# The attention projection as a third Strassen turn, and raw weight loads issued from GpSimd

## Chip, cores and metric

One core of a Trainium2 chip. The metric is the device time of one execution in microseconds (us). Engines: TensorE (PE), VectorE (DVE), ScalarE (ACT), GpSimd (POOL), and SyncE (SP), which issues DMAs.

## The reference

A decoder layer on 512 tokens of width 2048, in float32. Two branches read the normalised and modulated input: an attention over a sliding window (32 heads of 64), and a gated delta rule (32 value heads of 128). Cut to what matters here:

```python
    y_a = a_out @ w_o_swa                               # [512, 2048] @ [2048, 2048]
    ...
    y_b = o.reshape(B, T, DN_VAL).astype(x.dtype) @ w_o_dn   # [512, 4096] @ [4096, 2048]
    y = jax.nn.sigmoid(mg_a) * y_a + jax.nn.sigmoid(mg_b) * y_b
    return x + gate * (y @ w_out)                       # [512, 2048] @ [2048, 2048]
```

## The kernel before

**Precision.** Each float32 operand is split into a high part (a ScalarE cast, L61) and the rest (a VectorE subtraction, L62), and each product is three matmuls (`mm3`, L273 to L275). So a 128x128 by 128x512 step costs three matmuls.

**Weights.** All weights pass PE once, as a list of jobs of 1 MB (`plan`). A job is loaded into a raw buffer (`load_job`, L215), split in two halves of 128x1024 (`split_half`, tiles whi and wlo, three buffers of each), and used. A half that is done frees its buffer; at the next step (`pump`) the split of a further half and the load of a further job are put into the program.

**Order.** The program is written out in the order of PE's work. Beside it run generators: `go` steps one after so many pumps, `paced` steps one by a budget: each pump adds the budget, each step costs what it yields. The compiler then orders the instructions of each engine by this order and by when it expects them to be ready. `behind` keeps an instruction from being ordered ahead of the last matmul put in before it.

**Stages.** Start and norm; delta keys; attention; delta heads (16 of them, 40 pumps each, then three tiles of the merge gate); four more tiles of the merge gate; then the closing stages, which the change touches:

- *Delta projection* (`branch_b`). [512, 4096] times [4096, 2048] is taken as two turns (h = 0, 1) over halves of the inner width, each a [512, 2048] x [2048, 2048] product by one level of Strassen (Winograd's form): for each of two column halves n, seven products m1, m7, m5, m2, m6, m4, m3 (`PRODUCTS`). Each is four weight halves by two token blocks by two by three matmuls, 48 in all. It needs sums of quarters of the activations (the forms a11, s3, s1, a12, s2, a22, s4, each a pair of tiles of 8 KB per partition, in slots f0 to f4 and x0 to x3) and sums of quarters of the weights. `delta_forms` makes forms from `o_d`, direct into slots or by way of `b_d` and `form_load`. `delta_evict` combines the products on VectorE; the first turn stores to `yo_d`, the second adds `prev` from there, transposes each [128 tokens, 512] block by four PE transposes into `pty` (L320), multiplies with the gate (`th`, from `mb_d`) and stores to `yb_d`.
- *Weight sums* (`weight_sums`): the sums of quarters of w_o_dn (two sets, to `g_d`) and of w_out (one set, to `f_d`), paced beside the delta heads from head 3 on, with budget 2.0. Of each set, every half quarter takes four loads of 512 KB, four adds of 128x1024 on VectorE (L1328) and four stores.
- *Attention projection* (first part of `finish`): `attention_input` loads `ao_d` and splits it into hh and hl during the second turn; then 16 tiles of 128 channels by 512 tokens (`channel_tile`, 16 x 3 matmuls each, jobs os0 to os15). Each is gated with `ma_d`, `yb_d` is added, and the forms of the output projection are made from it in the same layout.
- *Output projection* (`output`): again seven products for each column half, then gate, residual and store. In PSUM the products rotate over six banks, and m7 has two.

All DMAs go out from SP, in the order of its instructions; a raw load waits on SP until its buffer is free. Raw buffers: two (`wraw`) and one more in the od jobs (`braw`), three more in the output projection (`oraw`). A raw load is L215; loads of prev and th are L1290 and L1293, of o L1204 and L1205.

Of the kernel before, what the change touches and what calls it, by code (L numbers as in the profile page):

```python
# [45 lines left out]
class Layer:  # L46
# [104 lines left out]
    def plan(self):  # L151
# [42 lines left out]
    def prime(self):  # L194
        self.job_load = self.half_split = self.half_used = 0
        self.raws, self.halves, self.due = {}, {}, []
        self.paused = False
# [4 lines left out]
    def load_job(self):  # L202
        j = self.job_load
        if j < len(self.jobs):
            src = self.jobs[j][1]
            if j == self.od1 and not self.paused:
                self.paused = True
                return
            if self.od0 <= j < self.od1:
                own = (j - self.od0) % 3 < 2  # L210
            else:
                own = j < self.out0 or (j - self.out0) % 5 < 2
            pool, tag = (self.wraw, "raw") if own else (self.oraw, "rawo")
            raw = pool.tile([P, 2048], F32, tag=tag, name="raw")
            self.nc.sync.dma_start(out=raw[:, : src.shape[-1]], in_=src)  # L215
# [107 lines left out]
    def build(self):  # L323
        tc, nc, a = self.tc, self.nc, self.a
        with ExitStack() as es:
# [6 lines left out]
            self.g_d = self.dram.tile([2, 2, 4, 2, P, 2048], F32, name="g_d")  # L332
# [22 lines left out]
            self.yb_d = self.dram.tile([KT, P, T], F32, name="yb_d")  # L355
# [6 lines left out]
            self.y_d = self.dram.tile([KT, P, T], F32, name="y_d")  # L362
# [3 lines left out]
            self.branch_b(work)  # L366
            self.finish(es, work, pm_es)
# [332 lines left out]
    def delta_heads(self):  # L700
        tc, nc = self.tc, self.nc
        with ExitStack() as sb:
# [423 lines left out]
    def branch_b(self, wk):  # L1126
        tc, nc, a = self.tc, self.nc, self.a
        forms = [p[1] for p in PRODUCTS]
        self.b_d = self.dram.tile([2, 2, P, 8, T], F32, name="b_d")
        self.yo_d = self.dram.tile([4, 4, P, T], F32, name="yo_d")  # L1130
        with ExitStack() as es:
            pf = self.pmb
            w = lambda name: wk.tile([P, T], F32, tag="w", name=name, bufs=9)
            self.gwk, self.gtag = wk, "w"
            fm = es.enter_context(tc.tile_pool(name="bf", bufs=1, side="right", reuse_waits="tile"))
            slots = [tuple(fm.tile([P, 8, 256], F32, name=f"f{i}{x}").bitcast(F32R) for x in "hl") for i in range(5)]
            fm.tile([P, 8], F32, name="alignb")
            self.oraw = es.enter_context(tc.tile_pool(name="braw", bufs=1, side="right", reuse_waits="tile"))
            A = [dict(zip(forms, slots)), {}]
# [5 lines left out]
            hx = ExitStack()  # L1145
            fx = hx.enter_context(tc.tile_pool(name="bx", bufs=1, reuse_waits="tile"))
            more = [tuple(fx.tile([P, 8, 256], F32, name=f"x{i}{x}").bitcast(F32R) for x in "hl") for i in range(4)]
            A[0].update(zip(forms[5:], more))
            for i, f in enumerate(forms[5:]):
                self.go(self.form_load(0, f, A[0][f]), 2 + 12 * i)  # L1150
            A[1].update(zip(forms, more[2:]))
            build = self.paced(self.delta_forms(wk, w, 1, A[1], 1), 1.0)
            ps, keep = {}, {}
            items = [(h, n, m) for h in range(2) for n in range(2) for m in range(7)]
            for h, n, m in items:
                name, form = PRODUCTS[m][:2]
                if (h, n, m) == (0, 1, 3):
                    self.drain_slow(build)
                k = [(0, 1, 3), (0, 1, 4), (0, 1, 5), (0, 1, 6), (1, 0, 0)]
                if (h, n, m) in k:  # L1160
                    k = k.index((h, n, m))
                    A[1][forms[k + 2]] = slots[k]
                    self.go(self.form_load(1, forms[k + 2], slots[k]), 2)
                if (h, n, m) == (1, 1, 2):
                    hx.close()
                    self.h_es = ExitStack()
                    self.hpool = self.h_es.enter_context(tc.tile_pool(name="h2", bufs=1))
                    self.hh = self.hpool.tile([P, KT, T], F32R, name="hh")
                    self.hl = self.hpool.tile([P, KT, T], F32R, name="hl")
                    ao = self.paced(self.attention_input(w), 1.0)  # L1170
                for t in range(2):
                    m7 = name == "m7"
                    ps[name, t] = pf.tile([P, T], F32, tag=f"y{t}", name=name, bufs=1) if m7 else self.product_bank(name)
                ah, al = A[h][form]
                for p in range(4):
                    hi, lo = self.half(f"od{h}{n}_{m}_{p // 2}")
                    for t in range(2):
                        for k in range(2):
                            kt, cols, tsl = 2 * p + k, slice(k * T, k * T + T), slice(t * P, (t + 1) * P)
                            self.mm3(ps[name, t], (ah[:, kt, tsl], al[:, kt, tsl]), (hi[:, cols], lo[:, cols]), kt == 0, kt == 7)  # L1180
                        if t:
                            self.half_done()
                        self.pump()
# [706 lines left out]
```

## Time and profile before

| | |
|---|---|
| time, median of 3 runs | 2791.58 us (2791.4 to 2793.72) |
| the profiled execution | 2789.26 us, of which the span 2787.2 us |
| granted TensorE clock | 0.999 |
| moved by DMA | 603.4 MB, mean 216 GB/s |
| second turn ends, attention projection starts | 2452.3 us |
| attention projection ends, output projection starts | 2630.3 us |

How to read the profile. In a list of stretches a row gives the stretch, its length, then for PE, PEld (weight load of PE), DVE, ACT and POOL the busy time and instructions, then the granted clock, the busy share of the DMA engines, and GB/s. In a list by tile or line a row gives line, engine, operation, output<-inputs and count; then either the least, median and longest duration in ns and the first and last start, or the busy time, the mean ns of one, and the idle time before with what ended it. Buffer numbers are left out of the names of rotating tiles (m is m1 to m7). A row of waits gives who waited for whom: us in all, times, and the longest. A timeline row gives start, duration, engine, line and operation, and in brackets the idle time before.

### The profile page before, as it was taken

To read this page: it belongs to the slowest core of one execution; us is meant where nothing else is said; L and a number is where in the kernel's file an instruction comes from. 1 tells how busy PE (TensorE), PEld (TensorE's weight loads), DVE (VectorE), ACT (ScalarE), POOL (GpSimd) and SP (SyncE) were. 2 spreads that over 40 slices of the span, in tenths; PEclk is the share of its full clock that TensorE was granted. 3 is DMA by queue.
4 is the path that set the end of the run, shared out by engine and by line. 5 is a ranking of instruction groups with operands and counts; after the bars stand their busy time and mean duration, and the time that the engine had idled before them with its cause. 6 is when DMAs were issued, how large, how long until landed. Compare 5 with 4: busy or idle time off the path is not lost.

```text
span 2787.2 us, 38923 instructions
## 1 busy us (share of the span) xinstructions
PE 2759.0 (99%) x14410; PEld 2256.5 (81%) x14410; DVE 1957.9 (70%) x3285; ACT 1207.4 (43%) x2508; POOL 137.9 (5%) x124
## 2 busy tenths in 40 slices
PE   8999999999999999999999999999999999999999
PEld 5788888877777788888888888888888888878887
DVE  7866986877758667788766666666657776764676
ACT  5555443244544433444534444444435454423443
POOL 0011110100100010000000000000000000000000
PEclk9999999999999999999999999999999999999999
DMA  9878764322253253367787776767647887885784
GB/s 403 353 235 243 269 229 131 112 93 93 87 144 112 101 166 116 116 214 243 258 268 242 241 243 242 239 235 248 227 162 266 310 298 245 284 272 189 245 315 168
DMA packets 228993, 603.40 MB, mean 216 GB/s; under 512 B 76706, under 2 KB 103074, under 8 KB 188482
## 3 DMA queue, kind: packets, MB, share of 16 engines
q1 hardware_dynamic: 228804, 600.93, 63.4%
q8 instruction: 113, 1.85, 0.3%
q14 instruction: 76, 0.62, 0.1%
HBM read 480.38 MB, written 118.24 MB: 215 GB/s over the span
## 4 chain that ended last, share of the span: by engine, by line
PE 90%; DMA 3%; DVE 3%; ACT 1%; issue 1%; SPq 0%; POOL 0%; DVEq 0%; POOLq 0%; ACTq 0%
PE mm L273 22%; PE mm L275 22%; PE mm L274 21%; PE m L274 5%; PE m L275 5%; PE m L273 5%; PE pod L1082 1%; PE pv L1063 1%; PE O L1597 1%; PE pp L1053 1%; PE pod L1078 1%; PE pod L1081 1%; DVE wlo L62 1%; DMA gw<-in_w_ada_gate 1%; DMA prev<-yo_d 1%
## 5 line engine op out<-in xcount | busy, mean ns | idle before, releaser
L273 PE MATMUL mm<-hh,whi 128*128 128x512 f32 x2784 | 1118.2, 402 | 0.0
L275 PE MATMUL mm<-hh,wlo 128*128 128x512 f32 x2784 | 1087.2, 391 | 1.9 <-DVE wlo L62 1.9
L274 PE MATMUL mm<-hl,whi 128*128 128x512 f32 x2784 | 1086.4, 390 | 0.0
L62 DVE TENSOR_TENSOR wlo<-raw,whi 128x1024 fp32r<-128x1024 f32 x516 | 636.1, 1233 | 463.8 <-ACT whi L61 450.7
L61 ACT CAST whi<-raw 128x1024 fp32r<-128x1024 f32 x516 | 541.1, 1050 | 884.2 <-PE mm L274 638.2
L273 PEld LDWEIGHTS mm<-hh,whi 128*128 128x128 f32 x2784 | 523.4, 188 | 115.4 <-issue 11.8
L275 PEld LDWEIGHTS mm<-hh,wlo 128*128 128x128 f32 x2784 | 522.5, 188 | 113.4 <-DVE wlo L62 2.5
L274 PEld LDWEIGHTS mm<-hl,whi 128*128 128x128 f32 x2784 | 523.5, 188 | 103.0 <-issue 1.4
L809 ACT ACTIVATE E<-E,neg_g 128x128 f32<-128x128 f32 x256 | 81.5, 391 | 99.3 <-POOL E L803 97.4
L1328 DVE TENSOR_TENSOR q<-q,q 128x1024 f32<-128x1024 f32 x96 | 120.1, 1251 | 1.4 <-DMA q<-in_w_od 1.4
L847 DVE TENSOR_TENSOR A<-A,atmp 128x62 f32<-128x62 f32 (+30 forms) x124 | 109.2, 881 | 0.4
L839 DVE TENSOR_TENSOR atmp<-A 128x62 f32<-128x62 f32 (+30 forms) x124 | 106.6, 860 | 0.4
L992 POOL TENSOR_TENSOR qe<-qe,yq 128x512 f32<-128x512 f32 x32 | 51.8, 1632 | 893.2 <-DMA qe<-eg_rows 553.2
L652 DVE SCALAR_TENSOR_TENSOR yv<-mm,convh,yv 128x511 f32<-128x511 f32 (+2 forms) x96 | 71.4, 744 | 10.2 <-ACT yv L649 9.5
L803 POOL TENSOR_SCALAR_AFFINE_SELECT E<-E 128x512 f32<-128x512 f32 x64 | 54.7, 863 | 436.5 <-DMA E<-g_rows 359.5
L1083 ACT COPY osb<-pod 128x256 f32<-128x256 f32 x64 | 23.7, 370 | 96.9 <-PE pod L1082 96.9
L1565 ACT ACTIVATE sm<-sm,mx,rs 128x128 f32<-128x128 f32 x128 | 61.5, 482 | 4.8 <-DVE mx L1560 4.4
L1065 ACT COPY vn<-pv 128x256 f32<-128x256 f32 x64 | 23.6, 369 | 73.0 <-PE pv L1063 73.0
L1056 DVE SCALAR_TENSOR_TENSOR r<-pp,neg_eg,vt 128x128 f32<-128x128 f32 x96 | 29.2, 345 | 34.3 <-PE pp L1053 34.1
L472 DVE SCALAR_TENSOR_TENSOR wa<-wa,silu_cb 128x2048 f32<-128x2048 f32 x22 | 50.1, 2285 | 2.6 <-DMA wa<-in_w_ada_ss 2.6
L657 ACT ACTIVATE th<-yv 128x512 f32<-128x512 f32 x32 | 20.2, 632 | 70.6 <-DVE yv L652 70.5
L1082 PE MATMUL pod<-vn,E 128*128 128x128 f32 x256 | 46.8, 275 | 0.0
(449 smaller groups left out, 3610.7 us busy)
## 6 DMA issues: line engine op xcount, KB each, us to landing
raw<-in_w_ch SPq DMA_DIRECT2D x158, 1024.0 KB
wa<-in_w_ada_ss SPq DMA_DIRECT2D x32, 1024.0 KB
q<-in_w_od SPq DMA_DIRECT2D x64, 512.0 KB
g_d<-q SPq DMA_DIRECT2D x64, 512.0 KB
raw<-g_d SPq DMA_DIRECT2D x32, 1024.0 KB
raw<-in_w_od SPq DMA_DIRECT2D x24, 1024.0 KB
gw<-in_w_ada_gate SPq DMA_DIRECT2D x16, 1024.0 KB
E<-g_rows SPq DMA_DIRECT2D x64, 256.0 KB
```

Of the source, the lines that this page charges most:

```text
L61: h = self.nc.scalar.copy(out=hi, in_=src)
L62: l = self.nc.vector.tensor_tensor(out=lo, in0=src, in1=hi.bitcast(F32), op=ALU.subtract)
L273: nc.tensor.matmul(ps, lhsT=wh, rhs=xh, start=first, stop=False)
L274: nc.tensor.matmul(ps, lhsT=wh, rhs=xl, start=False, stop=False)
L275: self.last_mm = nc.tensor.matmul(ps, lhsT=wl, rhs=xh, start=False, stop=last)
L652: nc.vector.scalar_tensor_tensor(out=y[:, s:], in0=ps[:, : T - s], scalar=w[:, j : j + 1], in1=y[:, s:], op0=ALU.mult, op1=ALU.add)
L809: self.nc.scalar.activation(E[:, c, :], E[:, c, :], AF.Exp, bias=self.neg_g[:, c, h : h + 1])
L839: eng.tensor_tensor(out=t, in0=A[:, m : m + 1, m + 1 :].to_broadcast([P, m, n]), in1=A[:, :m, m : m + 1].to_broadcast([P, m, n]), op=ALU.mult,
L847: self.behind(eng.tensor_tensor(out=A[:, :m, m + 1 :], in0=A[:, :m, m + 1 :], in1=t, op=ALU.add))
L1082: nc.tensor.matmul(po[:, e, :], lhsT=M[e][:, c, :], rhs=vn[:, e, :], start=c == 0, stop=True)
L1328: self.behind(nc.vector.tensor_tensor(out=q[f], in0=q[x], in1=q[y], op=ALU.add))
L1565: nc.scalar.activation(t, t, AF.Exp, scale=r[:, h : h + 1], bias=mx[:, h : h + 1], accum_out=den[:, h : h + 1])
```

## The change

The attention projection becomes a third turn (h = 2) of the delta projection: the same product loops, with weights w_o_swa and the forms made by `delta_forms` from `ao_d`. `branch_b` is now `projections`, and calls `output` at its end; `finish` and `attention_input` are gone. The third turn's blocks come out as [tokens, 512] and go through a new generator, `y_blocks`, which transposes, gates and adds as above and makes the forms of the output projection: written straight into slots where those are free, else stored to `c_d` and fetched with `y_half`. `weight_sums` has a fourth set (w_o_swa to `g_d[2]`), starts at head 1 with budget 1.0 and goes on with 2.4 from head 3. From the third od job on, raw loads are issued from GpSimd. In the second turn the loads of prev and th go out for both blocks at once, and four pumps pass before their use. The output projection takes its PSUM banks from the four that the turns use, and has two raw buffers of its own in place of three.

```diff
@@ plan
-        for half in range(2):
+        for half in range(3):
...
-        self.od1 = len(jobs)
-        jobs += [(f"os{j}", a["w_os"][j]) for j in range(KT)]
@@ load_job
-            if j == self.od1 and not self.paused:
-                self.paused = True
-                return
-            if self.od0 <= j < self.od1:
+            if j < self.od0:
+                own = True
+            elif j < self.out0:
                 own = (j - self.od0) % 3 < 2
             else:
-                own = j < self.out0 or (j - self.out0) % 5 < 2
-            pool, tag = (self.wraw, "raw") if own else (self.oraw, "rawo")
+                own = (j - self.out0) % 5 < 2
+            third = j < self.out0 or (j - self.out0) % 5 == 2
+            pool, tag = (self.wraw, "raw") if own else (self.braw if third else self.oraw, "rawo")
             raw = pool.tile([P, 2048], F32, tag=tag, name="raw")
-            self.nc.sync.dma_start(out=raw[:, : src.shape[-1]], in_=src)
+            (self.nc.sync if j < self.od0 + 3 else self.nc.gpsimd).dma_start(out=raw[:, : src.shape[-1]], in_=src)
...
-            if j == self.od0 + 1:
+            if j in (self.od0 + 1, self.out0 + 2, self.out0 + 3):
                 self.load_job()
@@ delta_heads
+                if g == 1:
+                    sums = self.paced(self.weight_sums(ws), 1.0)
                 if g == 3:
-                    sums = self.paced(self.weight_sums(ws), 2.0)
+                    sums[1] = 2.4
@@ branch_b -> projections
+            A[2].update(zip(forms, more[:2]))
+            A[3].update(zip(forms, slots[3:]))
+            places = {1: slots, 2: more[2:] + slots[:3]}
+            taken = {(2, 1, 1): ("s1", more[0]), (2, 1, 2): ("a12", more[1])}
+            taken.update({(2, 1, 5): ("s2", slots[0]), (2, 1, 6): ("a22", slots[1])})
...
+                        if h < 2 and (n, m) == (0, 0):
+                            build = self.paced(self.delta_forms(wk, w, h + 1, A[h + 1], 1), 1.0)
...
+                        if (h, n, m) in taken:
+                            self.y_half(*taken[h, n, m])
...
+            self.output(w, fx, A[3], slots[2])
+    def y_half(self, f, slot):
+        self.ydst[f] = slot
+        self.go(self.form_load(self.c_d[self.cforms.index(f)], slot, 4), 2)
@@ delta_evict
+        if h == 2:
+            yield from self.y_blocks(wk, w, pf, n, name, out)
+            return
+        loads = []
+        for c, t, src in out if h else ():
...
+        if loads:
+            yield 4
...
-            yield 3
             TT(out=src, in0=src, in1=prev, op=ALU.add)
...
-            nc.sync.dma_start(out=self.yb_d[4 * cc : 4 * cc + 4, :, tsl].rearrange("j p t -> p j t"), in_=th)
+            nc.sync.dma_start(out=self.yb_d[cc, t], in_=th.rearrange("p j t -> p (j t)"))
@@ y_blocks
+        for c, t, src in out:
...
+        yield 4
+        for t, src, y, b in blocks:
+            pt = pf.tile([P, 4, P], F32, tag="tp", name="pty", bufs=2)
+            self.transpose4(pt.rearrange("p j t -> p (j t)"), lambda j: src[:, j * P : (j + 1) * P])
+            yield 1
+            STT(out=y, in0=y, scalar=1.0, in1=pt.rearrange("p j t -> p (j t)"), op0=ALU.add, op1=ALU.mult)
+            TT(out=y, in0=y, in1=b, op=ALU.add)
+        yield 1
+        def put(f, t, src):
+            tsl = slice(t * P, (t + 1) * P)
+            if f in self.ydst:
+                ks = slice(4 * n, 4 * n + 4)
+                self.split(self.ydst[f][0][:, ks, tsl], self.ydst[f][1][:, ks, tsl], four(src))
+            else:
+                nc.sync.dma_start(out=self.c_d[self.cforms.index(f)][:, :, tsl], in_=four(src))
...
@@ weight_sums
-        sets = [(a["w_od"][0], self.g_d[0]), (a["w_od"][1], self.g_d[1]), (a["w_out"], self.f_d)]
+        sets = [(a["w_od"][h], self.g_d[h]) for h in range(3)] + [(a["w_out"], self.f_d)]
@@ output
-                    ps[name, t] = pf.tile([P, T], F32, tag=f"y{t}" if m7 else "r", name=name, bufs=1 if m7 else 6)
+                    ps[name, t] = pf.tile([P, T], F32, tag=f"y{t}", name=name, bufs=1) if m7 else self.product_bank(name)
...
-            if n == 0 and m in (2, 3):
-                kt = 4 * (m - 2) + p
-                nc.sync.dma_start(out=late[:, kt], in_=self.c_d[kt])
+            if (n, m, p) == (0, 0, 1):
+                self.y_half("s4", last)
...
-                    self.weight_tick()
+                self.pump()
```

More of the change, by code (lines that the diff above doesn't have):

```diff
@@ L1148, in branch_b @@
             A[0].update(zip(forms[5:], more))
             for i, f in enumerate(forms[5:]):
-                self.go(self.form_load(0, f, A[0][f]), 2 + 12 * i)
+                self.go(self.form_load(self.form_src(0, f), A[0][f]), 2 + 12 * i)
             A[1].update(zip(forms, more[2:]))
-            build = self.paced(self.delta_forms(wk, w, 1, A[1], 1), 1.0)
-            ps, keep = {}, {}
[L1154 to L1183, printed above, removed]
-                self.go(self.delta_evict(w, pf, h, n, name, dict(ps), keep), 1)
@@ L1232, in delta_forms, with form_src, form_load @@
         store()
[L1234 to L1243 removed]
+    def form_src(self, h, f):
+        if f == "a12":
+            rows = self.o_d[16 * h + 8 : 16 * h + 16] if h < 2 else self.ao_d[8:16]
+            return rows[:, :, 0:256].rearrange("k p t -> p k t")
+        x, c = {"s2": (0, 0), "s1": (0, 1), "s4": (1, 0), "a22": (1, 1)}[f]
+        return self.b_d[h, x][:, :, c * 256 : (c + 1) * 256]
+    def form_load(self, src, slot, n=8):
+        hi, lo = slot
+        self.behind(self.nc.sync.dma_start(out=lo[:, 0:n, :].bitcast(F32), in_=src))
+        for i in range(n // 4):
             yield 2 if i else 7
@@ L1282, in delta_evict @@
             yield 1
+        if h == 2:
[3 more added lines that the diff above has]
+        for c, t, src in out if h else ():
+            cc = 2 * c + n
+            prev, th = w("prev"), wk.tile([P, T], F32, tag="yh", name="th", bufs=4)
+            nc.sync.dma_start(out=prev, in_=self.yo_d[cc, t])
+            tsl = slice(t * P, (t + 1) * P)
+            th = th.rearrange("p (j t) -> p j t", t=P)
+            nc.sync.dma_start(out=th, in_=self.mb_d[4 * cc : 4 * cc + 4, :, tsl].rearrange("j p t -> p j t"))
+            loads.append((prev, th))
+        if loads:
+            yield 4
         for c, t, src in out:
@@ L1300, in delta_evict @@
             yield 2
-            nc.sync.dma_start(out=self.yb_d[4 * cc : 4 * cc + 4, :, tsl].rearrange("j p t -> p j t"), in_=th)
-    def attention_input(self, w):
-        for kt in range(KT):
-            raw = w("aoraw")
-            self.nc.sync.dma_start(out=raw, in_=self.ao_d[kt])
-            yield 1.2
-            self.split(self.hh[:, kt, :], self.hl[:, kt, :], raw)
-            yield 1.2
+            nc.sync.dma_start(out=self.yb_d[cc, t], in_=th.rearrange("p j t -> p (j t)"))
+    cforms = ["a11", "s3", "s1", "a12", "s2", "a22", "s4"]
@@ L1657, in output @@
-    def output(self, es, w, fx, A):
-        tc, nc, a = self.tc, self.nc, self.a
-        pf = es.enter_context(tc.tile_pool(name="pfo", bufs=1, space=PSUM, reuse_waits="tile"))
-        late = fx.tile([P, 8, 4, 256], F32, name="late")
-        for k, s in enumerate(("a22", "s4")):
-            A[s] = tuple(late[:, :, 2 * k + x, :].bitcast(F32R) for x in range(2))
-        self.oraw = es.enter_context(tc.tile_pool(name="oraw", bufs=3, reuse_waits="tile"))
-        for _ in range(3):
-            self.load_job()
+        pf = self.pmb
```

178 lines of the change are left out of this document (98 added, 80 removed).

## The prediction

> **What bounds the kernel now.** I read the page first: the engines' shares, the chain that ended last, the groups.
>
> ```profile
> span 2787.2 us, 38923 instructions
> PE 2759.0 (99%) x14410; PEld 2256.5 (81%) x14410; DVE 1957.9 (70%) x3285; ACT 1207.4 (43%) x2508; POOL 137.9 (5%) x124
> PE 90%; DMA 3%; DVE 3%; ACT 1%; issue 1%; SPq 0%; POOL 0%; DVEq 0%; POOLq 0%; ACTq 0%
> ```
>
> PE is busy 99% of the span and is 90% of the chain. So matmuls taken away are time taken away, as long as VectorE and the DMAs keep up; and a removed wait can give little, since all of PE's idle time is 28 us. Next, the closing stages one by one (busy time by stretch):
>
> ```profile
> core 0: us, PE busy (x) PEld busy (x) DVE busy (x) ACT busy (x) POOL busy (x), PEclk, DMA share, GB/s
> 2137.30:2292.20 154.90, 153.67 (x673) 126.10 (x672) 111.44 (x141) 79.05 (x93) 0.00 (x0) 1.00 0.87 304
> 2292.20:2452.30 160.10, 159.00 (x717) 130.26 (x716) 110.18 (x123) 71.81 (x79) 0.00 (x0) 1.00 0.80 266
> 2452.30:2630.30 178.00, 177.16 (x789) 145.79 (x788) 96.65 (x158) 55.83 (x87) 0.00 (x0) 1.00 0.66 218
> 2630.30:2787.20 156.90, 152.51 (x673) 125.94 (x671) 107.05 (x126) 62.89 (x67) 0.00 (x0) 1.00 0.72 257
> ```
>
> These are the two turns of the delta projection, the attention projection and the output projection. GpSimd does nothing in them; VectorE is at 72, 69, 54 and 68%. The stretches are cut where these rows (by tile) start:
>
> ```profile
> L273 PE MATMUL m<-whi,f0h x64: 392/392/397, 2137.3 to 2405.8; 128*128 128x512 f32 x64
> L273 PE MATMUL m<-whi,f1h x64: 392/392/394, 2148.3 to 2416.8; 128*128 128x512 f32 x64
> L273 PE MATMUL mm<-hh,whi x256: 388/389/500, 2452.3 to 2629.7; 128*128 128x512 f32 x128
> L273 PE MATMUL m<-whi,a11h x32: 389/389/390, 2630.3 to 2716.7; 128*128 128x512 f32 x32
> L273 PE MATMUL m<-whi,s3h x32: 389/389/389, 2641.2 to 2727.6; 128*128 128x512 f32 x32
> ```
>
> A Strassen product is 48 matmuls and follows the one before after 10.9 us (a11h to s3h), a pitch of 0.227 us (the 389 ns are latency); read from slots f0 to f4 it takes 11.0 us (f0h to f1h).
>
> **The change, part by part.** *1. Matmuls.* The attention projection is now 16 tiles x 16 x 3 = 768 matmuls: 768 x 0.2272 = 174.5 of its 178.0 us; the other 3.5 are late transposes and waits of the second turn, which stay. As a third turn it has 14 products, 8 from x slots and 6 from f slots: 8 x 10.9 + 6 x 11.0 = 153.2 us. **-21.3 us.**
>
> *2. Transposes.* The old form gave [channel, token] directly; the new one gives [token, channel], and each of 16 blocks is turned by four PE transposes. The second turn already does this (timeline of PE):
>
> ```profile
> 2471.80 0.40 PE L274 MATMUL mm<-hl,whi 128*128 128x512 f32 x1
> 2472.03 0.60 PE L320 MATMUL pty<-ident,m 128*128 128x128 f32 x4
> 2472.39 0.49 PE L275 MATMUL mm<-hh,wlo 128*128 128x512 f32 x1
> 2472.71 0.39 PE L273 MATMUL mm<-hh,whi 128*128 128x512 f32 x1
> ```
>
> From 2471.80 to 2472.71 stand two matmuls and one group: 0.91 - 2 x 0.227 = 0.46 us. 16 x 0.46 = **+7.3 us.**
>
> *3. Output projection.* Five of its seven forms come to lie in f slots, for both column halves: 10 products x 0.1 = **+1.1 us.** Its products rotate over four PSUM banks where they had six: the bank of m6 must be read out within one product (10.9 us) before m3; that takes 8 VectorE operations of 0.68, 5.5 us. I cost this at 0; without that cover the wait would be up to 2 us, twice.
>
> *4. Weight sums, in the delta heads.* A third matrix is summed: 32 more VectorE adds, 32 loads and 32 stores of 512 KB on SP, begun at head 1 (budget 1.0) and then run at 2.4 for 2.0. Rows: the adds by tile, heads before and with sums by stretch, one piece of the chain.
>
> ```profile
> L1328 DVE TENSOR_TENSOR q<-q,q x96: 1209/1217/2308, 1209.0 to 2036.7; 128x1024 f32<-128x1024 f32 x96
> 1139.00:1204.50 65.50, 65.50 (x378) 55.07 (x377) 48.23 (x79) 27.40 (x68) 4.57 (x4) 1.00 0.45 150
> 1204.50:1270.00 65.50, 64.03 (x369) 53.51 (x369) 55.04 (x86) 26.91 (x67) 4.95 (x4) 1.00 0.66 233
> 1270.00:1336.00 66.00, 65.46 (x377) 54.72 (x376) 57.51 (x102) 27.29 (x68) 5.37 (x4) 1.00 0.69 237
> 1533.00:1599.00 66.00, 66.00 (x383) 55.49 (x382) 44.01 (x75) 27.45 (x68) 6.06 (x4) 1.00 0.73 247
> 1296.62 7.28 DMA E<-g_rows
> ```
>
> 39 us more on VectorE, spread over a thousand. Later heads (1533) carry sums with PE full; only where sums and the triangular solve coincide (1204 to 1336, VectorE at 84 to 87%) is 0.5 to 1.5 us of a head lost, partly to a late E. The overlap grows from some four heads to six, and is denser. Bounds 0 and 7 (five heads at 1.5); I take **+1.5**, nearest to the row with 0.5. Does the sum end in time? One quarter costs 43 units of budget; 32 x 43 = 1376 against 80 + 13 x 40 x 2.4 + 24 x 2.4 = 1386: yes, just.
>
> *5. VectorE and ScalarE in the closing turns.* By form:
>
> ```profile
> L62 DVE TENSOR_TENSOR wlo<-raw,whi 128x1024 fp32r<-128x1024 f32 x56 | 68.4, 1222 | 39.1 <-ACT whi L61 38.9
> L62 DVE TENSOR_TENSOR hl<-aoraw,hh 128x512 fp32r<-128x512 f32 x12 | 7.9, 683 | 0.8 <-ACT hh L61 0.8
> L1210 DVE TENSOR_TENSOR s<-o 128x256 f32<-128x256 f32 x8 | 3.4, 422 | 6.2 <-DMA o<-o_d 6.2
> L62 DVE TENSOR_TENSOR f3l<-f3l,f3h 128x1024 fp32r<-128x1024 f32 x2 | 2.4, 1215 | 0.0
> ```
>
> Second turn: it loses the split of the attention input (-7.9) and gains the forms of the third turn, 8 x 6 operations like L1210 (+20.4) and some three form loads (+7.3): 110.2 -> 130 of 161 us, 81%. Third turn: 56 weight halves (68.4; the old stage had 32), 28 eviction adds, 32 operations of the y blocks, 34 combinations and splits at 0.68, and 4 half forms: 68.4 + 64.2 + 4.9 = 138, and 9 left over from the second turn, for 164 us; some 22 of it run into the output projection. ScalarE gets 24 more casts of 1.05 and stays under 60%. The nearest rows at such a load are the two heads above, which lost 0.5 and 1.5 of 65: over 161 us 1.3 to 3.6. I take **+1.5** for the second turn and **+2.5** for the third with its seam; bounds 0 and 11 (first rival).
>
> *6. Raw loads on GpSimd.* They leave SP, where each blocks what stands behind it (waits of the SP queue, then of the engines):
>
> ```profile
> SPq L215 <- DVE wlo L62: 171.9, 48, 6.5
> DVE m L1295 <- DMA prev<-yo_d: 3.0, 3, 2.0
> DVE c L1295 <- DMA prev<-yo_d: 2.5, 4, 0.8
> PE pty L320 <- DVE c L1295: 1.1, 2, 0.7
> PE m L274 <- DVE wlo L62: 1.2, 1, 1.2
> ```
>
> For 172 us SP stood still before a raw load until its buffer came free, with loads of prev, th and o behind it. They now go out at once, and prev and th come a pair at a time with four steps of cover in place of three. But PE waited little for this: **-2 us**, of at most 5.
>
> The price of a load issued by GpSimd is in no row, since GpSimd issues none. What it may cost is bounded by what covers it. Three buffers turn in the od jobs, and a job lasts 2 x 12 x 0.2272 = 5.45 us; of a buffer's 16.4 us some 5.0 lie between the first cast and the last subtraction. So a load may land up to 11.4 us after its issue. SP's nearest row:
>
> ```profile
> L1242 SPq DMA_DIRECT2D x0l<-b_d x1: 556/556/556, 2139.8 to 2139.8; - x1
> L61 ACT CAST x0h<-x0l x2: 1047/1050/1052, 2146.7 to 2149.1; 128x1024 fp32r<-128x1024 f32 x2
> ```
>
> The same 1 MB is read 6.9 us after its issue. I take that for GpSimd, and **0**; the other end is twice that, 13.8 us, (13.8 - 11.4) / 3 x 81 jobs = +65. The 28 jobs of the output projection have five buffers and more room.
>
> The Trainium skill (DMA: Bandwidth & Descriptors, Issuing engines are not separate DMA queues) says that DMAs from any engine share the same 16 DMA engines and that another issuer saves sequencer time alone. By that the move gives what the SP rows give and no bandwidth; the 2 us here agree with it.
>
> *Sum:* -21.3 + 7.3 + 1.1 + 1.5 + 1.5 + 2.5 - 2 = **-9.4 us.** The profiled execution took 2789.26 us (2787.2 and 2.1 around it), 2.3 below the median of the runs, 2791.58. Off the median: **2782.2 us.** A change of 0.2%, 5.6 us, is about what a measurement of this kernel can tell.
>
> **The rivals.** *VectorE clumps at the last seam (no change).* After the last m4 and m3 of the third turn some 30 operations of 0.68 and two form splits of 1.22 come due within about 11 steps of 1.36 us, beside 5.5 weight halves: 20.4 + 2.4 + 6.7 = 29.5 us of work in 15.0. The weight halves run two ahead, 5.5 us less the 2.3 of a cast and a subtraction: 3.2 us of cover. If the halves stand behind that work, PE waits 11.3 us in place of the 2.5: 2791. A burst of this kind, m6 of the first turn, in VectorE's timeline (first and last of 15 operations without a gap):
>
> ```profile
> 2195.33 0.69 DVE L1270 TENSOR_TENSOR u<-m,m 128x512 f32<-128x512 f32 x1 [2.62 <-DMA yo_d<-c]
> 2204.55 1.22 DVE L62 TENSOR_TENSOR wlo<-raw,whi 128x1024 fp32r<-128x1024 f32 x1
> ```
>
> For: after a late DMA it cost PE 1.2 (the wait on wlo above). Against: four of the 15 are weight halves, put between the others.
>
> *The loads from GpSimd come too late (slower).* At 13.8 us: 2782 + 65 = 2847; it decides from 12.0 us on, where 81 x 0.6 / 3 = 16 us eat the gain and the bound. For: no row shows that engine issuing. Against: it is idle here, and 81 loads have 5.1 us each over SP's 6.9.
>
> *VectorE holds GpSimd's issue up (slower).* Where VectorE runs without a gap, as for the 10.4 us of that burst, an issue that needs the gap waits 5.2 us on average and at worst 10.4, and lands at 12.1 to 17.3, say 14.9, 3.5 us too late; two m6 bursts in each of three turns: +21, 2803. The Trainium skill (SBUF — State Buffer, SBUF: two separate sides) tells of such a lock, by VectorE operations in a 2-port mode. Against: wlo takes 1222 ns for 1024 elements, about one element a cycle of that engine, no double rate.
>
> *The change does not do what it says* has no place: matmul counts are fixed by the code.
>
> **How the numbers follow.** Forecast 0.70; clumps at the seam (or heads that cost the upper bound) 0.14, counted as no change; late loads 0.10; held-up issue 0.06. The likeliest case reaches from 2774 (no stalls, -5 for SP: -17.9) to 2786. With the no-change case up to 2797 the range holds 0.84; the slower rivals stay out. Faster by over 0.2%: 0.70; within: 0.14; slower: 0.16.
>
> **What would show it.** Third turn about 164 us from its first product to the output's first, with 64 more transposes; output projection 157 to 160; second turn 161; PE's idle time no more than 35 us in all. Right on step 6: no wait of SP on wlo, and no wait of a cast on a raw load. Wrong, if casts of whi wait on raw (late loads), if PE waits on wlo for several us around the start of the output projection (clumps), if heads 1 to 6 take over 67 us each, or if the last f_d store is later than the first turn.

## The result and the profile after

| | median us | against the kernel before |
|---|---|---|
| before (5 runs beside it) | 2793.72 | |
| after (5 runs) | 2827.39 | 1.0128, 95% interval 1.0109 to 1.0147 |

The change made the kernel slower by 1.3%, some 36 us (the two medians alone lie 33.7 us apart, 1.2%); 2782.2 was predicted, and the range ended at 2797. The profiled execution took 2825.38 us, of which the span is 2823.6, 36.4 above the span of before.

From the page of the kernel after: TensorE's row, the shares of the chain, the two larger groups of raw loads that GpSimd issues (count, KB, median us to landing). In the changed kernel the three matmuls are L270 to L272, the transposes into `pty` L317 and the addition of prev L1320:

```profile
PE 2764.2 (98%) x14378; PEld 2254.8 (80%) x14378; DVE 2044.3 (72%) x3362; ACT 1235.9 (44%) x2517; POOL 204.9 (7%) x233
PE 83%; DMA 7%; DVE 6%; issue 2%; ACT 2%; SPq 0%; POOL 0%; DVEq 0%; POOLq 0%; ACTq 0%
raw<-g_d POOLq DMA_DIRECT2D x47, 1024.0 KB, 6.6
raw<-in_w_od POOLq DMA_DIRECT2D x34, 1024.0 KB, 7.1
```

TensorE's share of the chain fell from 90 to 83%, and DMA's rose from 3 to 7: it waits for transfers. These are not the loads on GpSimd, which land after 6.6 and 7.1 us, as assumed (6.9), and the longest of all 109 after 9.6. The stages, in the form of the rows of before:

```profile
0.00:2145.04 2145.04, 2119.62 (x11563) 1730.09 (x11563) 1565.42 (x2771) 938.82 (x2183) 147.53 (x125) 1.00 0.64 219
2145.04:2307.39 162.35, 156.05 (x673) 127.41 (x672) 113.60 (x146) 80.39 (x95) 14.34 (x27) 0.98 0.84 296
2307.39:2486.96 179.57, 167.15 (x721) 135.51 (x720) 122.49 (x160) 73.72 (x85) 14.88 (x28) 0.95 0.83 284
2486.96:2658.29 171.33, 164.38 (x746) 134.05 (x744) 121.14 (x139) 75.68 (x82) 15.94 (x30) 0.98 0.82 286
2658.29:2823.60 165.31, 157.01 (x683) 127.78 (x681) 121.70 (x148) 67.33 (x73) 12.22 (x23) 0.99 0.61 210
```

Up to the first turn 7.7 us more than before; first turn +7.4, although its work is the same; second turn +19.5; third turn 6.7 less than the attention projection; output projection +8.4. TensorE stands still for 34.0 us in the four closing stages (length less busy time), before for 7.6. In all four the granted clock is under 1.00, where before it was 1.00 everywhere. VectorE is busy for 70, 68, 71 and 74% of them: it is not out of time, it stands still at the wrong moments. One of these, in the first turn: the chain (start, us), and the timelines of ScalarE, VectorE and TensorE:

```profile
2211.48 9.02 DMA b_d<-o
...
2220.51 6.28 DMA o<-o_d
...
2226.91 0.44 DVE o L1228
```

```profile
2215.37 0.41 ACT L61 CAST x2h<-o 128x256 fp32r<-128x256 f32 x1 [3.26 <-DMA o<-o_d]
2215.83 0.41 ACT L61 CAST x3h<-s 128x256 fp32r<-128x256 f32 x1
2216.14 1.04 ACT L61 CAST whi<-raw 128x1024 fp32r<-128x1024 f32 x1
2221.76 0.41 ACT L61 CAST x2h<-o 128x256 fp32r<-128x256 f32 x1 [4.57 <-DMA o<-o_d]
2222.07 1.04 ACT L61 CAST whi<-raw 128x1024 fp32r<-128x1024 f32 x1
```

```profile
2226.91 0.43 DVE L1228 TENSOR_TENSOR o<-o,o 128x256 f32<-128x256 f32 x1 [3.96 <-DMA o<-o_d]
...
2227.72 1.22 DVE L62 TENSOR_TENSOR wlo<-raw,whi 128x1024 fp32r<-128x1024 f32 x1
```

```profile
2223.17 0.51 PE L270 MATMUL m<-whi,f0h 128*128 128x512 f32 x1 [0.67 <-ACT whi L61]
2228.99 0.80 PE L271 MATMUL m<-wlo,f0h 128*128 128x512 f32 x1 [5.32 <-DVE wlo L62]
2229.58 0.63 PE L272 MATMUL m<-whi,f0l 128*128 128x512 f32 x1
```

A tile of the pool "w" is stored (9.0 us), then loaded with the next o (6.3). ScalarE takes its instructions in order, and here each cast of a weight half stands behind a form's cast (x2h) that waits for such an o: one half in 5.9 us, where TensorE uses one in 2.7. The row of the cast shows no wait of its own: it ran as soon as x2h was through. VectorE is held in the same way, and that is what TensorE feels: the cast of the half was done at 2223.1, but on VectorE a sum of forms that waited 4.0 us for an o stood ahead of its subtraction, and TensorE waits 5.3 us for this wlo. Then the next matmuls follow each other at 0.43 us in place of 0.23; the granted clock of that stretch:

```profile
2209.00:2223.00 14.00, 13.19 (x57) 10.25 (x56) 8.69 (x15) 4.45 (x7) 1.06 (x2) 1.00 0.90 299
2228.00:2234.80 6.80, 5.81 (x17) 4.68 (x18) 6.77 (x12) 3.22 (x4) 0.54 (x1) 0.64 0.57 169
2234.80:2241.00 6.20, 6.20 (x29) 5.07 (x27) 3.65 (x5) 2.58 (x3) 0.53 (x1) 1.00 1.03 358
```

In the closing stages of after, six such periods at half clock add up to 34 us by the trace's clock records (four of 6.8, two of 3.4). In 7.7 us of these TensorE was waiting anyway, so some 13 us of matmul time are lost by them; before there was none.

### The profile page after: what moved, and what is told of

The parts are those of the page before. It is cut to its first block, busy times and chain, and to the rows that moved or that the text cites. A ratio compares the mean times of both kernels' runs of the same rounds, so it can differ in the third digit from the quotient of the medians.

```text
span 2823.6 us, 39123 instructions
## 1 busy us (share of the span) xinstructions
PE 2764.2 (98%) x14378; PEld 2254.8 (80%) x14378; DVE 2044.3 (72%) x3362; ACT 1235.9 (44%) x2517; POOL 204.9 (7%) x233
## 4 chain that ended last, share of the span: by engine, by line
PE 83%; DMA 7%; DVE 6%; issue 2%; ACT 2%; SPq 0%; POOL 0%; DVEq 0%; POOLq 0%; ACTq 0%
PE mm L270 19%; PE mm L272 19%; PE mm L271 19%; PE m L271 5%; PE m L272 5%; PE m L270 5%; DVE wlo L62 1%; PE pod L1079 1%; DMA E<-g_rows 1%; PE pv L1060 1%; PE O L1680 1%; DMA b_d<-o 1%; DMA o<-ao_d 1%; PE pod L1075 1%; PE pp L1050 1%
## 5 line engine op out<-in xcount | busy, mean ns | idle before, releaser
L270 PE MATMUL mm<-hh,whi 128*128 128x512 f32 x2528 | 1019.8, 403 | 0.1
L272 PE MATMUL mm<-hh,wlo 128*128 128x512 f32 x2528 | 988.2, 391 | 1.9 <-DVE wlo L62 1.9
L271 PE MATMUL mm<-hl,whi 128*128 128x512 f32 x2528 | 987.7, 391 | 0.0
L62 DVE TENSOR_TENSOR wlo<-raw,whi 128x1024 fp32r<-128x1024 f32 x540 | 664.0, 1231 | 437.4 <-ACT whi L61 420.6
L61 ACT CAST whi<-raw 128x1024 fp32r<-128x1024 f32 x540 | 565.5, 1049 | 864.4 <-PE mm L271 550.9
L270 PEld LDWEIGHTS mm<-hh,whi 128*128 128x128 f32 x2528 | 475.9, 188 | 105.5 <-issue 11.8
L272 PEld LDWEIGHTS mm<-hh,wlo 128*128 128x128 f32 x2528 | 475.3, 188 | 104.1 <-DVE wlo L62 2.5
L271 PEld LDWEIGHTS mm<-hl,whi 128*128 128x128 f32 x2528 | 476.2, 188 | 92.9 <-issue 1.4
L1411 DVE TENSOR_TENSOR q<-q,q 128x1024 f32<-128x1024 f32 x128 | 158.7, 1240 | 4.8 <-DMA q<-in_w_od 3.8
L271 PE MATMUL m<-wlo,f0h 128*128 128x512 f32 x128 | 51.3, 401 | 5.3 <-DVE wlo L62 5.3
```

What stands on the lines that cost most here:

```text
L61: h = self.nc.scalar.copy(out=hi, in_=src)
L62: l = self.nc.vector.tensor_tensor(out=lo, in0=src, in1=hi.bitcast(F32), op=ALU.subtract)
L270: nc.tensor.matmul(ps, lhsT=wh, rhs=xh, start=first, stop=False)
L271: nc.tensor.matmul(ps, lhsT=wh, rhs=xl, start=False, stop=False)
L272: self.last_mm = nc.tensor.matmul(ps, lhsT=wl, rhs=xh, start=False, stop=last)
L1411: self.behind(nc.vector.tensor_tensor(out=q[f], in0=q[x], in1=q[y], op=ALU.add))
```

## The experiments

The runs went through four questions: which part of the change costs, whether it is the queue or the order, what the sums in the heads cost, and where the third turn's gain went. The stage lengths below are from the rows of each run's own profile; each run's ratio is to runs of the kernel before on the same chip (medians of 2789.8 to 2791.4), and differences between runs of different chips are taken from the ratios (0.001 is 2.8 us).

### Which part: e1, e2

e1 is the change with one line undone, e2 the kernel before with that line alone.

```diff
e1 (to the kernel after)
-            (self.nc.sync if j < self.od0 + 3 else self.nc.gpsimd).dma_start(out=raw[:, : src.shape[-1]], in_=src)
+            self.nc.sync.dma_start(out=raw[:, : src.shape[-1]], in_=src)
e2 (to the kernel before): the same two lines the other way round
```

> The change with the one line of the raw loads undone: every raw load is issued from SyncE again. Theory A (the raw loads on GpSimd's queue go out as soon as their buffer is free and land among SyncE's small transfers, which come 8 to 10 us late; VectorE and ScalarE wait for these in order, and the halves of the weights stand behind them): the first turn goes from 162 us back to about 155, the second from 180 to about 163, the output from 165 to about 158, and the time from 2827 to about 2800. Theory C (the third turn's forms and its loads in the second turn are the cost, whoever issues the raw loads): first turn 160 or more, second turn 175 to 180, time 2815 to 2827. A third possibility, that the loads on SyncE now stand behind its waits for buffers being stored: stalls on the halves, time above 2827.

> The kernel before with the second part of the change alone: raw loads of the closing stages from GpSimd, projection still by the plain attention stage. Theory A: the first turn goes from 155 to about 162 and the whole from 2792 to 2800 to 2815. Theory C: no change, 2790 to 2794.

e1: 2790.40 us, 1.0003 (0.9993 to 1.0013). e2: 2818.06 us, 1.0103 (1.0088 to 1.0118). e1's stages from the first turn on, then e2's first two turns:

```profile
2141.51:2296.50 154.99, 153.72 (x673) 126.12 (x672) 111.44 (x141) 79.15 (x93) 0.00 (x0) 1.00 0.87 305
2296.50:2462.35 165.85, 162.29 (x723) 132.64 (x721) 125.63 (x166) 76.23 (x90) 0.00 (x0) 0.98 0.91 310
2462.35:2623.38 161.03, 161.03 (x745) 132.98 (x743) 121.77 (x141) 74.22 (x81) 0.00 (x0) 1.00 0.88 306
2623.38:2785.89 162.51, 155.43 (x683) 126.64 (x681) 120.56 (x145) 67.14 (x73) 0.00 (x0) 1.00 0.63 214
```

```profile
2137.35:2298.42 161.07, 156.26 (x673) 127.12 (x672) 111.94 (x141) 79.48 (x93) 14.29 (x27) 0.99 0.84 295
2298.42:2477.72 179.30, 164.63 (x721) 133.91 (x720) 111.60 (x126) 73.85 (x82) 14.30 (x27) 0.97 0.73 244
```

The line of the raw loads alone costs 28 us in the kernel before and 35 in the changed one (1.0128 less 1.0003; 37.7 by the spans). With loads from SyncE the first turn is back at 155.0. e2 shows 161.1 and 179.3 without a third turn, near after's 162.4 and 179.6: theory C, that the third turn's forms are the cost, fell as the main cause, since 28 of the 35 us come without them. Theory A's numbers missed too: e1 came 10 us under the 2800 expected, e2 3 us over the 2815. Strassen alone (e1) neither gains nor loses; the third turn itself is at 161 where the attention projection took 178.

### Queue or order: e6, e8, e10, e11

e1 and the kernel after differ in more than the queue. The compiler orders each engine's instructions by when it expects them to be ready, and with the raw loads out of SyncE's queue that order comes out differently on ScalarE, VectorE, SyncE and TensorE. e6 holds the form work back in the order, e8 makes the packets of GpSimd's loads smaller.

```diff
e6 (to the kernel after; so too for s3, the first difference, and the addition of prev)
-                self.split(direct[f][0][:, kt, :], direct[f][1][:, kt, :], src)
+                for i in self.split(direct[f][0][:, kt, :], direct[f][1][:, kt, :], src):
+                    self.behind(i)
e8 (to the kernel after)
-            (self.nc.sync if j < self.od0 + 3 else self.nc.gpsimd).dma_start(out=raw[:, : src.shape[-1]], in_=src)
+            for c in range(4 if j >= self.od0 + 3 else 0):
+                s = slice(512 * c, 512 * c + 512)
+                self.nc.gpsimd.dma_start(out=raw[:, s], in_=src[:, s])
+            if j < self.od0 + 3:
+                self.nc.sync.dma_start(out=raw[:, : src.shape[-1]], in_=src)
```

> The changed kernel, raw loads on GpSimd, with one edit to the order: the operations of delta_forms that read a loaded o (casts, subtractions, the first two sums) and the addition of prev may not be ordered ahead of the last matmul put in before them. Theory B (the loads cost so much because the compiler, which sees a second queue, puts this form work ahead of weight halves on ScalarE and VectorE, and these then stand behind a transfer of 6 to 9 us): first turn from 162 to about 157, second from 180 to 165 to 170, time from 2827 to 2795 to 2808. Theory A (the packets of the second queue delay SyncE's transfers, in whatever order): 2820 or more.

> The changed kernel with each raw load on GpSimd cut into four loads of 512 columns, so packets of 2 KB in place of 8 KB. Theory A (SyncE's small packets take turns with the large packets of the other queue): SyncE's transfers land earlier, and the first turn falls from 162 towards 155, the time to about 2805 to 2815. Theory B: no gain, 2820 to 2830, or slower by the four issues of 0.53 us each.

e6: 2817.09 us, 1.0082 (1.0058 to 1.0105), between the two forecasts. The profiled run, at 2804.94, is 12 us under the other three. In it the first turn takes 155.9, as without GpSimd, the second 174.4 of 179.6, the third 163.7. This speaks for the order in the first turn; in the second, TensorE now waited in its transposes (pty) for additions of prev. e8: 2821.70 us, 1.0108 (1.0085 to 1.0130), a gain of 6 that the intervals do not tell from none; the first turn took 158.2, the second 178.0. So the size of the packets is at most a small part of the cause, and e8, too, was ordered anew by the compiler.

e10 and e11 separate the two. The instructions of the closing stages are chained, engine by engine, in the order that the compiler gave the other kernel.

```diff
+    for names in ...:              # one list for each engine
+        here = [made[f"I-{n}"] for n in names if f"I-{n}" in made]
+        for one, two in zip(here, here[1:]):
+            tc.add_manual_dep(two, one.name, mybir.DependencyInfo(mybir.DependencyClass.NoSync, ...), reason="pin")
e10: the kernel after, with the lists of e1 (PE, DVE, ACT, and SP without its raw loads)
e11: e1, with the lists of the kernel after (PE, DVE, ACT)
```

> The changed kernel, raw loads on GpSimd, with the instructions of TensorE, VectorE, ScalarE and SyncE (but for the raw loads) pinned from the first turn on to the order that the compiler gave the kernel with raw loads from SyncE. So only the queue of the raw loads differs from that kernel. Theory B (the order costs, not the queue): closing stages as there, time 2786 to 2795. Theory A (the queue costs: SyncE's transfers land later beside it): 2805 to 2825. In between, the two parts share it in the proportion measured.

> The other corner: raw loads from SyncE, with TensorE, VectorE and ScalarE pinned to the order of the changed kernel. Theory B: slow although nothing goes out from GpSimd, 2810 to 2830. Theory A: 2786 to 2800.

| ratio to before (interval), median us | order of e1 | order of the kernel after |
|---|---|---|
| raw loads from SyncE | e1: 1.0003 (0.9993 to 1.0013), 2790.40 | e11: 1.0211 (1.0188 to 1.0234), 2849.67 |
| raw loads from GpSimd | e10: 1.0005 (0.9995 to 1.0015), 2792.59 | after: 1.0128 (1.0109 to 1.0147), 2827.39 |

e10's first two turns, then e11's:

```profile
2144.30:2299.91 155.61, 153.70 (x674) 126.11 (x672) 111.16 (x141) 78.97 (x93) 14.29 (x27) 1.00 0.84 302
2299.91:2465.72 165.81, 161.32 (x722) 132.17 (x721) 125.75 (x166) 76.67 (x90) 14.86 (x29) 0.99 0.90 314
```

```profile
2142.84:2326.52 183.68, 160.86 (x674) 128.07 (x672) 112.38 (x145) 79.92 (x95) 0.00 (x0) 0.95 0.77 261
2326.52:2517.06 190.54, 169.52 (x722) 135.15 (x720) 122.59 (x160) 73.71 (x87) 0.00 (x0) 0.96 0.80 266
```

The order of e1 takes 34 of the 35 us back with every raw load from the fourth od job on still on GpSimd (the first three stay on SyncE in the changed kernel); the other order costs 59 us with none there. Theory B stands, theory A fell as the cause. Two things stay open. e11 lies 20 us over its forecast: the order of after is worse still with the loads on SyncE, so order and queue do not simply add. And e10 holds SyncE's order too, e11 does not, so what SyncE's order contributes is not told apart. ScalarE's timeline in e10, at the place shown of after:

```profile
2215.05 0.41 ACT L61 CAST x2h<-o 128x256 fp32r<-128x256 f32 x1 [3.68 <-DMA o<-o_d]
2215.36 1.05 ACT L61 CAST whi<-raw 128x1024 fp32r<-128x1024 f32 x1
2216.32 0.40 ACT L61 CAST x3h<-s 128x256 fp32r<-128x256 f32 x1
2216.62 1.04 ACT L61 CAST whi<-raw 128x1024 fp32r<-128x1024 f32 x1
2218.53 1.05 ACT L61 CAST whi<-raw 128x1024 fp32r<-128x1024 f32 x1 [0.86 <-PE m L272]
2221.19 1.05 ACT L61 CAST whi<-raw 128x1024 fp32r<-128x1024 f32 x1 [1.61 <-PE m L272]
2226.14 1.05 ACT L61 CAST whi<-raw 128x1024 fp32r<-128x1024 f32 x1 [3.90 <-PE m L272]
2227.10 0.40 ACT L61 CAST x2h<-o 128x256 fp32r<-128x256 f32 x1
```

The o comes as late here (3.7 us of waiting), but five halves are cast ahead of the next x2h, where in after it was one. TensorE waits 1.9 us for wlo in place of 5.3, and the clock stays full. The loads on GpSimd do touch SyncE's transfers, but that is not what costs. Worked out from the landing records (issue to the last landing), the median for o<-o_d in the first turn is 6.5 us before, 5.8 in e2 and after, 6.1 in e10; the longest went from 7.7 before to 11.0 in e2, 10.3 in after and 10.2 in e10. So the slowest come some 3 us later beside the other queue, in e10 as much as in after, and of these two only the order of after lets it reach TensorE in full. In e11 the longest is 8.6, and the loss is the greatest of the four. That the compiler puts the form work further ahead when the raw loads are on another queue is read from the two orders; why it does so lies in when it expects transfers to land, which no trace shows.

### The sums in the heads: e3, e5, e9, e12, e16

e3 and e5 put the weight sums behind the solve (e3 with GpSimd's loads, e5 with SyncE's), e12 begins them at head 5. e12 also changes a `yield 4` before the use of prev to 6. e9 has e6's edit, loads from SyncE, and head 6 with budget 3.7. e16 leaves out the sums of the third matrix, so it does not compute the layer and only prices them.

```diff
-                if g == 1:
-                    sums = self.paced(self.weight_sums(ws), 1.0)
-                if g == 3:
-                    sums[1] = 2.4
+                if g == 6:                                        # e12: g == 5
+                    sums = self.paced(self.weight_sums(ws), 3.3)  # e9: 3.7, e12: 3.0
e16 (to e1; sums from head 3 with budget 2.0)
-                        src = ... self.g_d[half, n, f, i]
+                        src = ... self.g_d[min(half, 1), n, f, i]
-        sets = [(a["w_od"][h], self.g_d[h]) for h in range(3)] + [(a["w_out"], self.f_d)]
+        sets = [(a["w_od"][h], self.g_d[h]) for h in range(2)] + [(a["w_out"], self.f_d)]
```

> The change with the weight sums begun at head 6 instead of head 1, at a budget of 3.3 us instead of 1.0 and 2.4, so that none of them lies beside the solve. Theory D (the 7.75 us that the stages up to the closing ones took longer come from the sums' VectorE work and transfers beside the solve): the stages up to the closing ones go from 2145 to about 2138, time from 2827 to about 2820. Rival (twice the sums packed into two heads are dense enough to hold VectorE up there): heads 6 and 7 give the same 5 to 8 us back, time 2825 to 2830.

> Both edits: raw loads from SyncE and the sums from head 6. If A and D hold and add: about 2793. If only A: about 2800. If neither: 2820 to 2827.

> All raw loads from SyncE, form work kept behind, and the weight sums begun at head 6 with budget 3.7 (at 3.3 they ended too near the closing stages: one stall of 2.5 us and its half clock at their start). If the heads' loss goes (4 us of it) and theory B holds: 2778 to 2783. If the sums at 3.7 are too dense for VectorE: 2788 to 2795.

> All raw loads from SyncE, the weight sums begun at head 5 with budget 3.0 (none beside the solve but at its end), and six pumps in place of four between the loads of prev and th and their use. If the heads' loss of 4 us is the overlap of sums and solve, the first turn starts at 2137 to 2139 in place of 2141.5; if the wait of 3.7 us in the second turn hangs on prev, that turn takes 157 to 159 in place of 163. Both: 2780 to 2784; neither: 2790.

> All raw loads from SyncE, and the sums of the third weight matrix left out: the third turn loads those of the second in their place, and the sums begin at head 3 with budget 2.0 as in the kernel before. So only the price of the third set goes. If it is the 4 us by which the first turn started later: 2786, with the first turn at 2137 to 2138. If that later start was chance of one run: 2790.

| run | median us | ratio (interval) | what came of the heads |
|---|---|---|---|
| e3 | 2822.00 | 1.0117 (1.0098 to 1.0135) | the first six heads 391.8 us (after 401.7, before 394.2), the nine behind them 3.5 more than before; first turn as if from 2144.4 |
| e5 | 2794.65 | 1.0013 (1.0004 to 1.0022) | the same, as if from 2143.9; TensorE waits 2.3 us there |
| e9 | 2859.40 | 1.0236 (1.0216 to 1.0256) | heads 8 to 14 take 71 to 81 us each |
| e12 | 2790.69 | 0.9998 (0.9989 to 1.0008) | first turn starts at 2143.3; second turn 163.7, with no wait over 1.5 us left in it |
| e16 | 2785.86 | 0.9983 (0.9974 to 0.9992) | first turn starts at 2137.7 |

(A product of the first turn stands ahead of the last gate tile in e3 and e5; "as if from" is the second product's start less 11.0.)

e9's head 9, and the stretch up to the first turn in e16:

```profile
1642.81:1719.77 76.96, 71.84 (x369) 58.37 (x368) 49.96 (x80) 28.49 (x74) 5.11 (x4) 0.96 0.83 287
```

```profile
0.00:2137.70 2137.70, 2116.28 (x11562) 1728.51 (x11563) 1532.30 (x2739) 938.02 (x2183) 137.90 (x124) 1.00 0.60 204
```

Theory D fell. In the kernel after the loss does lie beside the solve (401.7 us for the first six heads, before 394.2). But out of the solve's way the sums cost as much later: in e3, e5 and e12 the first turn comes some 6 us or more after that of before. e5's 2794.65 is what theories A and D together forecast, by luck: e1 gave 2790 without moving the sums. e12 came out at the 2790 forecast for the case that neither of its two conditions holds, e9 far over both of its forecasts. The price belongs to the third set, wherever it is put: without it the first turn starts at 2137.7 (before: 2137.3; with it and the change's own pace 2141.5 to 2145.9 in ten profiles), and e16 is 0.0020, 5.6 us, under e1 (either ratio is uncertain by 0.0010). Part of the spread is no price of the sums: the first head starts between 1042.9 and 1045.6 us, though none of the edits touches the stages ahead of it. From there to the first turn it is 1094.2 us before, 1094.8 in e16, and 1098.1 to 1100.6 with the third set (e9 left aside). At 3.7 the heads collapse. VectorE is idle for a third of e9's head 9, so it is not VectorE that is full; what fails there was not followed further.

### Where the third turn's gain went: e7, e13, e14, e15

In e1 two stalls are left. VectorE at the first, then TensorE at the first and at the second (the start of the output projection):

```profile
2359.05 0.43 DVE L1224 TENSOR_TENSOR s<-o 128x256 f32<-128x256 f32 x1 [2.12 <-DMA o<-ao_d]
...
2365.95 2.35 DVE L62 TENSOR_TENSOR wlo<-raw,whi 128x1024 fp32r<-128x1024 f32 x2
```

```profile
2367.22 0.79 PE L271 MATMUL m<-wlo,f4h 128*128 128x512 f32 x1 [3.49 <-DVE wlo L62]
...
2650.22 0.50 PE L271 MATMUL m<-wlo,x0h 128*128 128x512 f32 x1 [2.39 <-DVE wlo L62]
2650.56 0.39 PE L272 MATMUL m<-whi,x0l 128*128 128x512 f32 x1
```

At the first, s waits 2.1 us for an o, then fourteen operations of forms and of the eviction of m6 (6.9 us) go ahead of two weight halves. e7 is e1 with e6's edit. e13 is e1 with its own order pinned and five instructions moved; e14 has that order with loads from GpSimd; e15 is e13 with two more places.

```diff
e13: VectorE and ScalarE, in the list of e1
+ wlo, whi (one half) ahead of s and x0h, which wait for o;  + wlo into the burst behind it
+ two wlo into the burst at the start of the output projection
e15: and
+ pty (four transposes) 18 matmuls later on PE;  + wlo ahead of the addition of prev on VectorE
```

> The same edit to the order with all raw loads from SyncE (the kernel of 2790). There one wait of this kind is left, 3.7 us in the second turn, and about as much again by the half clock behind it. Theory B: second turn from 163 to about 157, time 2783 to 2786. Rival (form work put later comes due in one piece at the end of the second turn): 2790 or more.

> All raw loads from SyncE, the order pinned to that kernel's own (2790), but for five places: before the wait on o in the second turn (3.7 us) one cast and one subtraction of a weight half are put ahead of the operations that wait, another subtraction into the burst behind them, and at the start of the output projection two subtractions into the burst there (2.6 us). If these two stalls and the half clock behind the first are what the third turn's gain was lost to: the second turn 7 us shorter, the output projection 2.5, time 2780 to 2783, faster than both kernels. If the waits only move to the next half: 2787 to 2791.

> The same order, SyncE's too, with the raw loads on GpSimd. If the queue has no price of its own: within 3 us of e13. If leaving SyncE brings the relief that the prediction put at 2 us (at most 5): 2 us under e13.

> The order of e13 with two more places moved: the transposes that waited 3.7 us for the addition of prev stand 18 matmuls later on TensorE, and a weight half ahead of that addition on VectorE. If the second turn's loss is this one late stretch, wherever it shows: the turn about 7 us shorter (3.7 of waiting and what the half clock costs behind it), time 2779 to 2782. If it moves on again to the next transposes: 2785 to 2788.

e7: 2789.96 us, 0.9995 (0.9986 to 1.0005), and 166.4 for the second turn: theory B's gain did not come. The stall stays (3.9 us), by this reading because the burst, not only the wait, holds the half. e13: 2787.35, 0.9988 (0.9979 to 0.9997): the second stall went, output 159.9 in place of 162.5; the first only moved, and the second turn stayed at 165.7:

```profile
2373.76 0.69 PE L317 MATMUL pty<-ident,c 128*128 128x128 f32 x4 [3.48 <-DVE c L1320]
```

e14: 2791.64, 1.0000 (0.9992 to 1.0009), 4.3 us over e13 where it was to stay within 3; in its profile the same transposes wait 5.3 us. e15: 2788.26, 0.9990 (0.9981 to 0.9999). No stall of over 2 us is left in its second turn, but the turn is 1 us shorter than in e1, not 7: TensorE stands still for 3.9 us in five waits of 0.2 to 1.7, where in e1 it was one of 3.5. So that the loss is one late stretch fell as well. Its stages from the second turn on:

```profile
2299.71:2464.53 164.82, 160.97 (x722) 130.40 (x721) 125.76 (x166) 76.22 (x90) 0.00 (x0) 1.00 0.91 313
2464.53:2625.56 161.03, 161.03 (x744) 132.98 (x743) 121.43 (x141) 74.19 (x81) 0.00 (x0) 1.00 0.88 305
2625.56:2785.42 159.86, 155.14 (x683) 126.72 (x681) 120.44 (x145) 67.04 (x73) 0.00 (x0) 1.00 0.64 217
```

From the first turn's start to the end e15 takes 640.6 us, before 649.9: 9.3 less. But the first turn starts 7.5 later in this profile (2144.8 against 2137.3). So the best versions, e13 and e15, are 0.1% faster than the kernel before, 3 us where 8 to 12 were expected.

## Why the prediction was wrong, step by step

*What failed: step 6.* It put the move of the raw loads at -2, with a price of 0 for the queue; it cost 35. The working weighed the wait on SyncE, the issue and the landing, and each was about right: 6.6 and 7.1 us to landing, 0.53 us of GpSimd for an issue, the longest landing 9.6 against the 11.4 that it allowed, no cast that waited on a raw load for over a microsecond. It took the order of all other engines as given. The rows in its own fence could have warned: 172 us of waiting on SyncE, and TensorE hardly noticed, so the order of before suited these waits. The compiler made a new order for the new queue, with form work ahead of weight halves on engines that go in order, and transfers of 6 to 9 us then reached TensorE. Both slower rivals on GpSimd (late loads, an issue held up) fell with these landings; the real one was not on the list. The nearest was the clumping, weight halves behind form work, but at the last seam alone and counted as no change. The relief of 2 us did not come even at equal order: e10 is 0.0002 above e1, within its uncertainty, and e14 4.3 us above e13, at the edge of what the two intervals tell apart. That the loads share the same DMA engines whoever issues them, as the Trainium skill has it (DMA: Bandwidth & Descriptors, Issuing engines are not separate DMA queues), agrees with this: 305 and 310 GB/s in e1's first two turns, 302 and 314 in e10's.

*Steps 1 and 2: right in sum.* Second and third turn together took 338.1 before; -21.3 + 7.3 + 1.5 gave 325.6 (328.1 with the 2.5 of the third turn and its seam); e1 took 326.9, e15 325.9. The split was off: 165.9 and 161.0 in e1 for 161 and 164. The third turn holds 18 groups of transposes, some of them the second turn's (in e15 744 instructions less 672 matmuls are 72 transposes), and 153.2 + 18 x 0.46 = 161.5 covers the 161.0; of the 3.5 us that were to stay nothing else shows.

*Step 3 and the seam.* Output 157 to 160 was predicted; e15 159.9. The wait by clumping at the last seam exists, at 2.4 us, not the 11 of that rival.

*Step 4: mis-sized.* +1.5 was taken, within 0 to 7; it is 5.6 by the ratios (e1 less e16) and 4 to 6 from the first head to the first turn. The term was sized by the overlap with the solve. That is where the loss lies in the kernel after, but not why it comes: it stayed when the sums left the solve.

*Step 5: mis-sized.* The second turn's +1.5 was 5.7 in e1: 2.5 us more of TensorE standing still (3.6 for 1.1), some 2.7 by the half clock behind the stall, and one group of transposes more (48 transposes for 44, 0.46 us). Without that stall it was still 4.7 in e15 and 3.6 in e12. What makes VectorE late there in one place or another was not followed.

Without step 6 the terms gave 2784; e1's ratio off the same median gives 2792. Of the 8 us some 4 are the heads; the rest is about what the two stalls of e1 cost, since e15, nearly without them, is at 2789 off the same median.

## What to carry to other kernels

Where a compiler orders instructions by expected readiness, moving DMAs to another queue can change the order on every engine, as here; compare the two orders before costing the move, and pin the old order to measure the queue alone. On an engine that goes in order, look at what stands behind each wait for a transfer: keep the work that feeds the bounding engine ahead of it (here one weight half between two such waits was too little, and five cost TensorE 1.9 us in place of 5.3). Waiting on a queue that nobody notices may be what the rest of the order rests on: taking it away is no gain by itself.

## What the runs showed of the hardware

A stall of TensorE has a second price, and where it falls decides on it. The granted clock goes by fixed windows: in each of the 17 profiles all stretches of half clock begin at whole multiples of 3.41 us from one another. Set beside TensorE's idle time in these windows (closing stages, up to the window in which the last matmul ends), a window at full clock with 1.9 us or more of idle time was followed by half clock 39 times of 39, one with 1.6 to 1.9 us 3 times of 13, one with less never. A window at half clock with 0.9 us or more of idle time was followed by another, 18 times of 18 in the profiles from 200 us on.

So equal stalls have different prices. The 3.5 us of e1 fell on two windows, 2.1 and 1.4 us of idle time, and half clock lasted 6.8 us; the 3.5 us of e13 lay almost wholly in one, and it lasted 3.4. The stall at the start of the output projection, the same 2.4 us in twelve kernels, left the clock full in seven (in e1, above, it is split into 1.35 and 1.04 us) and brought 3.4 us of half clock in five (in e16 it lies in one window; in e10 1.9 us of it do); e10's rows:

```profile
2653.59 0.50 PE L271 MATMUL m<-wlo,x0h 128*128 128x512 f32 x1 [2.40 <-DVE wlo L62]
2653.93 0.40 PE L272 MATMUL m<-whi,x0l 128*128 128x512 f32 x1
...
2655.10 0.60 PE L272 MATMUL m<-whi,x0l 128*128 128x512 f32 x1
2655.50 0.63 PE L270 MATMUL m<-whi,x0h 128*128 128x512 f32 x1
```

The Trainium skill (TensorE: Matmul & The Clock Gate, Part 1: The HAM clock gate) tells of a free-running window of some 3.4 us, of which one idle makes the clock half. The length and the free running of the window agree with the 3.41 us here. That a whole window must be idle does not: 1.9 us of idle time in it were enough.
